# Hybrid RWKV-7 / RG-LRU / retention block: the projections alternate between two PSUM banks throughout the mixers

## Chip, core and metric

One NeuronCore of a Trainium2 chip runs the whole kernel as a single launch. The metric is the device time of one launch in microseconds (us), as a median over runs. The engines are named as in the profile: PE (TensorE; PEld is its weight load), DVE (VectorE), ACT (ScalarE), POOL (GpSimd) and SP (the sync engine, which here only issues DMAs).

## What is computed

One layer on 512 tokens of width 2048, in float32:

```python
h = rms_norm(x, norm1_g)
proj = h @ w_in                      # split by columns among three groups of heads
y_a = rwkv7_mixer(...)               # 12 heads x 64, delta-rule state, decay from the data
y_b = rglru_mixer(...)               # 512 channels, width-4 conv, gelu gate
y_c = retention_mixer(q, k, v, g, cos, sin, log_gamma, gn_g)   # 6 heads, qk 64, v 128, swish gate
x = x + concat(y_a, y_b, y_c) @ w_out
h = rms_norm(x, norm2_g)
x = x + (silu(h @ w_gate) * (h @ w_up)) @ w_down
return rms_norm(x, final_norm_g)
```

## The kernel before

**Precision and the unit of work.** Every large product is made in three matmuls: `split` (L157) writes a high half of an operand with ACT (the CAST of L158) and the rest with DVE (the TENSOR_TENSOR of L141), and `mm3` (L161) issues high by high, high by low and low by high as L162, L163 and L164. HH and HL are the two halves of h, resident in SBUF. Weights come through RAW (two slots of 128x1024, loaded by SP), and from there through WH and WL (four slots of 128x512 each).

**Projections.** `proj` (L270) makes one 128-column tile of `h @ w_in` for all 512 tokens: four weight pieces, 48 matmuls of 128x512 into one PSUM bank. The caller then reads the bank with DVE (`bank * rB`). Which bank it is, L272 decides. `ret_qk` (L731) makes the tiles cq and ck, `ret_gate` (L697) a tile cg.

**Value projections.** `ret_v` (L768), called with 0, 1 and 2, makes the values of two retention heads: 192 matmuls of 128x256, half of them into bank 0 and half into bank 7 (`vb`, L770). ACT then takes them out in eight activations of 128x128, four from each bank, into `vT`. With argument 0 these go to the slots 46 and 47 of the tile M; slot 46 also holds the decay table `DT[1]` (L721), which `ret_scores(1)` and its neighbours read on DVE. M, 45 slots of 128x512, holds nearly everything that the mixers keep.

**The third RWKV group.** `rwkv_inverse(2)` (L504) inverts 64 small triangular matrices with a chain of 62 dependent DVE instructions and a copy (L518), and passes the result through DRAM: SP writes scrN (L520) and scrX (L521) and reads them back into M (L523 and L530). `rwkv_join(2)` (L533) multiplies the parts with 32x32 matmuls on PE, with ACT copies between (L543, L552). `rwkv_chain(2)` (L556) then runs eight chunks, each a sequence from PE to DVE to PE to ACT and DVE to PE (L573, L145, L167, L581, L585, L594, L596, L600). The chunks hang on each other; other matmuls fill PE between their parts.

**What sets the order.** The steps are written in the order of the list SCHEDULE (L57). Its end reads: ... inverse 2, ..., qk 0, scores 0, join 2, qk 1, scores 1, chain 2, **value 0, qk 2**, out 2, heads 0, scores 2, **cg 4, value 1**, store 2, norm 0, **cg 5**, store 2 (first half), **value 2**, heads 1, ... From that order, from `tc.high_priority()` blocks and from which instructions it finds ready, a scheduler makes one list for each engine when the kernel is built. On the chip each engine works through its list in that order, and waits where an operand or a buffer isn't free. Within a bank the scheduler keeps a new group of matmuls behind the reads of the group before.

The two lines that decide the bank:

```python
o = bank[1 if ring["cv"] else nxt("proj", 2)]     # L272, in proj
ring["cv"] = 1                                    # first line of ret_v
```

So until `ret_v(0)` the tiles alternate between banks 0 and 1; from then on (cq 2, ck 2, cg 4, cg 5) all use bank 1, while the value projections use 0 and 7.

Of the kernel before, what the change touches and what calls it, by code (L numbers as in the profile page):

```python
# [98 lines left out]
def hybrid_block(ctx: ExitStack, tc: tile.TileContext, A: dict, out: bass.AP, dbg=None):  # L99
# [19 lines left out]
    bank = [pp.tile([128, 512], F32, name=f"bank{i}") for i in range(8)]  # L119
# [37 lines left out]
    def split(raw, hi, lo):  # L157
        S.copy(out=hi, in_=raw)  # L158
        tt(lo, raw, hi.bitcast(F32), SUB)

    def mm3(o, wh, wl, xh, xl, first, last, **kw):  # L161
        PE.matmul(o, wh, xh, start=first, stop=False, **kw)  # L162
        PE.matmul(o, wh, xl, start=False, stop=False, **kw)  # L163
        PE.matmul(o, wl, xh, start=False, stop=last, **kw)  # L164
# [24 lines left out]
    ring = {"sm": 0, "gn": 0, "raw": 0, "w": 0, "mm": 0, "proj": 0, "cv": 0}  # L189

    def nxt(k, n):
        v = ring[k]
        ring[k] = (v + 1) % n
        return v
# [74 lines left out]

    def proj(name, j, between=None):  # L270
        idx = W_IDX[(name, j)]
        o = bank[1 if ring["cv"] else nxt("proj", 2)]  # L272
        for half in range(2):
            with tc.high_priority() if idx > 1 else ExitStack():
                r = RAW[:, nxt("raw", 2), :]
                nc.sync.dma_start(out=r, in_=A["w_in"][idx, half])
                pcs = []
                for u in range(2):
                    w = nxt("w", 4)
                    split(r[:, u * 512:(u + 1) * 512], WH[:, w, :], WL[:, w, :])  # L280
                    pcs.append(w)
            if half and between:
                between()
            for u in range(2):
                w = pcs[u]
                for kk in range(4):
                    k = half * 8 + u * 4 + kk
                    cs = slice(kk * 128, (kk + 1) * 128)
                    mm3(o, WH[:, w, cs], WL[:, w, cs], HH[:, k, :], HL[:, k, :], k == 0, k == KT - 1)
        return o  # L290

    tok = []
    first = proj("k", 0, lambda: tok.append(head_rsqrt_stat(acc, c("mD"), 1, mmb, eps=NORM_EPS)))
    rT = drv[:, 108:112]
    V.tensor_copy(out=rT, in_=tok[0])
# [89 lines left out]
    def rwkv_proj(pr):  # L385
        sr, sk, sv = rkv(pr)
        with tc.high_priority() if pr > 1 else ExitStack():
            (G if pr else nc.sync).dma_start(out=LW, in_=A["lora"][pr, :, 0:256])
        shift(sk, proj("k", pr) if pr else first, "mu_k", pr)
        shift(sr, proj("r", pr), "mu_r", pr)  # L390
        shift(sv, proj("v", pr), "mu_v", pr)
# [967 lines left out]
```

## Time and profile before

| | us |
|---|---|
| median of 3 runs | 2301.12 (2299.13 to 2305.68) |
| the profiled execution | 2305.94 |
| its span, first to last instruction | 2304.0 |

The profile is of that one execution: a page with the busy time of each engine, and views of the trace by stretch, by line and in order of time. A row in order of time gives the start, the duration, the engine, the line, the operation, and in brackets the idle time ahead of it and what ended that. Matmuls overlap, so a matmul's duration is longer than its share of PE's time; the distance from start to start is what counts. A float32 matmul that isn't split (L167, L573, L596) leaves two records for one instruction. PEclk is the granted clock of TensorE; 1.00 is 2.4 GHz and 0.50 is 1.2 GHz.

### The profile page before, as it was taken

To read this page: it belongs to the slowest core of one execution; us is meant where nothing else is said; L and a number is where in the kernel's file an instruction comes from. 1 tells how busy PE (TensorE), PEld (TensorE's weight loads), DVE (VectorE), ACT (ScalarE), POOL (GpSimd) and SP (SyncE) were. 2 spreads that over 40 slices of the span, in tenths; PEclk is the share of its full clock that TensorE was granted. 3 is DMA by queue.
4 is the path that set the end of the run, shared out by engine and by line. 5 is a ranking of instruction groups with operands and counts; after the bars stand their busy time and mean duration, and the time that the engine had idled before them with its cause. 6 is when DMAs were issued, how large, how long until landed. Compare 5 with 4: busy or idle time off the path is not lost.

```text
span 2304.0 us, 29339 instructions
## 1 busy us (share of the span) xinstructions
PE 2261.3 (98%) x11005; PEld 1861.6 (81%) x11005; DVE 1632.9 (71%) x2749; ACT 1000.7 (43%) x1646; POOL 22.0 (1%) x59
## 2 busy tenths in 40 slices
PE   8999999999999999999999999999999999999998
PEld 7878777777888888788888888888888788888887
DVE  7778689688646554878777777878787455565555
ACT  5563465454225543444444444444444432232234
POOL 0000000000000000000000000000000000000000
PEclk9999999999989999999999999999999999999999
DMA  5324233324413454334333423342331544454332
GB/s 201 103 81 113 76 94 89 108 67 128 111 52 120 149 177 145 114 126 148 110 110 119 154 94 128 110 142 93 127 132 37 174 152 134 135 162 122 114 106 74
DMA packets 119070, 272.50 MB, mean 118 GB/s; under 512 B 35904, under 2 KB 42304, under 8 KB 107536
## 3 DMA queue, kind: packets, MB, share of 16 engines
q1 hardware_dynamic: 108208, 250.46, 34.5%
q10 hardware_dynamic: 8448, 12.59, 1.5%
q0 software_dynamic: 2272, 7.58, 1.1%
q8 instruction: 86, 1.41, 0.3%
q14 instruction: 56, 0.46, 0.1%
HBM read 241.36 MB, written 27.66 MB: 117 GB/s over the span
## 4 chain that ended last, share of the span: by engine, by line
PE 82%; DVE 13%; ACT 2%; issue 2%; DMA 1%; ACTq 0%; DVEq 0%; SPq 0%
PE bank L162 25%; PE bank L163 25%; PE bank L164 25%; PE bank L167 5%; DVE RB L141 4%; DVE WL L141 3%; DVE M L141 2%; DVE HL L141 1%; PE bank L573 1%; PE bank L1054 1%; DVE G L150 1%; PE bank L596 1%; DVE E L141 1%; ACT WH L158 1%; DVE M L150 0%
## 5 line engine op out<-in xcount | busy, mean ns | idle before, releaser
L162 PE MATMUL bank<-HH,WH 128*128 128x512 f32 x992 | 396.8, 400 | 13.4 <-ACT HH L153 5.8
L158 ACT CAST WH<-RAW 128x512 fp32r<-128x512 f32 (+1 forms) x339 | 216.9, 640 | 427.3 <-PE bank L163 365.7
L164 PE MATMUL bank<-HH,WL 128*128 128x512 f32 x992 | 394.4, 398 | 0.0
L163 PE MATMUL bank<-HL,WH 128*128 128x512 f32 x992 | 394.0, 397 | 0.0
L141 DVE TENSOR_TENSOR WL<-RAW,WH 128x512 fp32r<-128x512 f32 (+1 forms) x339 | 240.5, 710 | 130.5 <-ACT WH L158 126.7
L158 ACT CAST WH<-RB 128x1024 fp32r<-128x1024 f32 x191 | 201.2, 1055 | 269.4 <-PE bank L164 251.2
L141 DVE TENSOR_TENSOR WL<-RB,WH 128x1024 fp32r<-128x1024 f32 x191 | 233.1, 1221 | 110.9 <-ACT WH L158 109.7
L162 PEld LDWEIGHTS bank<-HH,WH 128*128 128x128 f32 x992 | 188.3, 190 | 53.4 <-ACT HH L153 5.8
L141 DVE TENSOR_TENSOR X<-X,bank 128x512 f32<-128x512 f32 (+1 forms) x178 | 115.9, 656 | 160.9 <-PE bank L164 159.9
L163 PE MATMUL bank<-GLo,WH 128*128 128x512 f32 x576 | 224.2, 389 | 0.0
L164 PE MATMUL bank<-GH,WL 128*128 128x512 f32 x576 | 224.2, 389 | 0.0
L162 PE MATMUL bank<-GH,WH 128*128 128x512 f32 x576 | 224.2, 389 | 0.0
L164 PEld LDWEIGHTS bank<-HH,WL 128*128 128x128 f32 x992 | 188.1, 190 | 38.9 <-issue 1.4
L163 PEld LDWEIGHTS bank<-HL,WH 128*128 128x128 f32 x992 | 188.3, 190 | 38.2 <-issue 1.4
L163 PE MATMUL bank<-WL,HH 128*128 128x512 f32 (+1 forms) x604 | 216.8, 359 | 0.0
L162 PE MATMUL bank<-WH,HH 128*128 128x512 f32 (+1 forms) x604 | 216.8, 359 | 0.0
L164 PE MATMUL bank<-WH,HL 128*128 128x512 f32 (+1 forms) x604 | 216.2, 358 | 0.0
L141 DVE TENSOR_TENSOR HL<-RB,HH 128x1024 fp32r<-128x1024 f32 (+2 forms) x127 | 128.6, 1027 | 56.5 <-ACT HH L158 55.7
L162 PE MATMUL bank<-WH,FAH 128*128 128x512 f32 x412 | 162.5, 395 | 3.8 <-ACT WH L158 3.8
L158 ACT CAST HH<-RB 128x1024 fp32r<-128x1024 f32 (+1 forms) x99 | 102.5, 1037 | 140.0 <-PE bank L164 126.7
L164 PE MATMUL bank<-WH,FAL 128*128 128x512 f32 x412 | 161.9, 393 | 0.0
L163 PE MATMUL bank<-WL,FAH 128*128 128x512 f32 x412 | 161.7, 392 | 0.0
(239 smaller groups left out, 3801.4 us busy)
## 6 DMA issues: line engine op xcount, KB each, us to landing
RB<-in_w_gu_dram SPq DMA_DIRECT2D x77, 1024.0 KB, 4.8
RAW<-in_w_in_dram SPq DMA_DIRECT2D x76, 512.0 KB, 3.6
RAW<-in_w_dn_dram SPq DMA_DIRECT2D x100, 256.0 KB, 2.7
RW<-in_w_dn_dram SPq DMA_DIRECT2D x76, 256.0 KB, 2.6
RAW<-in_w_out_dram SPq DMA_DIRECT2D x32, 512.0 KB, 3.6
RAW<-in_w_gu_dram SPq DMA_DIRECT2D x11, 1024.0 KB, 4.9
hscr<-H ACTq DMA_DIRECT2D x44, 256.0 KB, 2.2
FT<-hscr SPq DMA_DIRECT2D x40, 256.0 KB, 3.0
```

The source lines that it names most:

```text
L141: (eng or V).tensor_tensor(out=o, in0=a, in1=b, op=op)
L150: V.scalar_tensor_tensor(out=o, in0=a, scalar=s, in1=b, op0=op0, op1=op1, **kw)
L158: S.copy(out=hi, in_=raw)
L162: PE.matmul(o, wh, xh, start=first, stop=False, **kw)
L163: PE.matmul(o, wh, xl, start=False, stop=False, **kw)
L164: PE.matmul(o, wl, xh, start=False, stop=last, **kw)
L167: PE.matmul(o, l, r, start=start, stop=stop)
L573: PE.matmul(F[:, q, hv[e]], LS[e][:, ch, :], VS[:, ch, hv[e]], start=(q == 0 and e == 0), stop=True, skip_group_check=(q > 0 or e > 0))
L596: PE.matmul(F[:, q, :], P_[q][1][:, ch, :], ZBq[:, q, :], start=False, stop=True, skip_group_check=True)
L1054: PE.transpose(b[:, 128 * t:128 * t + 128], (G_, X_)[t // 2][:, t % 2, 128 * f:128 * f + 128], ident)
```

## The change

Projections always take the next of banks 0 and 1. `ring["cv"]` is still set, and nothing reads it any more.

```diff
     def proj(name, j, between=None):
         idx = W_IDX[(name, j)]
-        o = bank[1 if ring["cv"] else nxt("proj", 2)]
+        o = bank[nxt("proj", 2)]
         for half in range(2):
```

34 tiles are made ahead of `ret_v(0)`, an even number, so that now cq 2 takes bank 0, ck 2 bank 1, cg 4 bank 0 and cg 5 bank 1. No instruction is added or removed. The scheduler, though, makes other lists of them from the end of `ret_v(0)` to the end of the mixers. Up to there all lists are the same.

**Place 1, the end of the value projections of call 0.** In the rows, bank7 with 128x256 is the value projection, 128x512 with HH or HL first is a projection (bank1: cq 2, ck 2, cg 4), and 32x32 is `rwkv_join(2)`. PE's list before:

```order
L164 MATMUL bank7_88<-WH_77,HL_80 128x256
L162 MATMUL bank1_82<-HH_79,WH_77 128x512
L163 MATMUL bank1_82<-HL_80,WH_77 128x512
L164 MATMUL bank1_82<-HH_79,WL_78 128x512
...
L162 MATMUL bank7_88<-WH_77,HH_79 128x256
L163 MATMUL bank7_88<-WL_78,HH_79 128x256
...
L167 MATMUL bank3_84<-M_101 32x32 x8
L167 MATMUL bank2_83<-M_101 32x32 x8
```

Between the first and the last of these rows stand 144 matmuls into bank 1 (three whole tiles) and 4 of the value projection of call 1. PE's list now (zn, ZB and VSt are the chunk chain's tiles):

```order
L164 MATMUL bank7_88<-WH_77,HL_80 128x256
L167 MATMUL bank3_84<-M_101 32x32 x8
L167 MATMUL bank2_83<-M_101 32x32 x8
...
L167 MATMUL bank2_83<-M_101 128x128 x4
L167 MATMUL bank5_86<-zn_109,M_101 128x128
L167 MATMUL bank5_86<-M_101 128x128 x2
L162 MATMUL bank0_81<-HH_79,WH_77 128x512
L163 MATMUL bank0_81<-HL_80,WH_77 128x512
L164 MATMUL bank0_81<-HH_79,WL_78 128x512
L596 MATMUL bank4_85<-ZB_113,M_101 128x128 x2
L573 MATMUL bank6_87<-VSt_112,M_101 128x64 x4
```

The join follows the value projection directly. The 96 matmuls of cq 2 and ck 2 stand among the chunks of the chain, the 48 of cg 4 and all 192 of the value projection of call 1 behind the chain; before, 48 of the latter stood ahead of the chain, 140 within it and 4 behind. Six products of `ret_heads(0)` (64x128) and eight of `ret_scores(2)`, which stood among the first two chunks, stand behind the chain too, with three transposes (L760).

ACT's list now at the same place, with the activations that take `ret_v(0)`'s results out of banks 7 and 0:

```order
L158 CAST WH_77<-RAW_76 128x512 x5
L153 ACTIVATE M_101,SM_107<-bank7_88,drv_71 128x128 x4
L543 COPY M_101<-bank3_84 32x256
...
L552 ACTIVATE M_101<-bank2_83 32x8x32
L153 ACTIVATE M_101,SM_107<-bank0_81,drv_71 128x128 x2
...
L153 ACTIVATE M_101,SM_107<-bank0_81,drv_71 128x128 x2
L585 COPY ZB_113<-bank5_86 64x2x64 x2
```

Bank 7 is taken out ahead of the join's first copy, bank 0 among and behind the join's last ones. In the list of before the activations of bank 0 stand at the same place, with 12 more casts of weights (RAW to WH) ahead of the join.

**Place 2, the inverse.** The small DVE instructions `M<-M 64x...` are the inverse, `WL<-RAW,WH` are the splits of projection weights, and `M<-bank_82,rB` is the read of a finished tile. A piece of DVE's difference:

```order
 L141 TENSOR_TENSOR M<-M 64x11x21 x2
 L141 TENSOR_TENSOR M<-M 64x12x20 x2
-L141 TENSOR_TENSOR WL<-RAW,WH 128x512
 L141 TENSOR_TENSOR M<-M 64x13x19 x2
 L141 TENSOR_TENSOR M<-M 64x14x18 x2
-L141 TENSOR_TENSOR M<-M 64x15x17
-L141 TENSOR_TENSOR WL<-RAW,WH 128x512
-L141 TENSOR_TENSOR M<-M 64x15x17
+L141 TENSOR_TENSOR M<-M 64x15x17 x2
```

From the row 64x11x21 to the inverse's copy (L518), 13 instructions of 128x512 that belong to the projections (eight splits, two reads of banks, three of the rotary step) have left; nothing stands between the inverse's instructions there now.

SP's difference, from the reads of the inverse's input on (L276 and L774 load weights, L743 is the rotary step's shuffle):

```order
 L509 DMA M<-scrA 32x32x32 x2
-L276 DMA RAW<-in_w_in_dram 128x1024 x4
-L743 DMA M<-M 32x512
-L276 DMA RAW<-in_w_in_dram 128x1024
-L743 DMA M<-M 32x512 x3
-L774 DMA RAW<-in_w_cv_dram 128x1024
-L743 DMA M<-M 32x512
-L774 DMA RAW<-in_w_cv_dram 128x1024
+L276 DMA RAW<-in_w_in_dram 128x1024 x3
+L521 DMA scrX<-M 64x1024
 L520 DMA scrN<-M 32x1024
```

Behind L520 the list now goes on with the eight L530 and the two L523, where before two L774 and two more L743 stood among them. One L276 (first half of cg 4) and everything after it now comes behind the inverse's DMAs.

## Rows read from the trace of the kernel before

**Rows 1.** The page's head: span, and PE's busy time, share, instructions.

```profile
span 2304.0 us, 29339 instructions
PE 2261.3 (98%) x11005; PEld 1861.6 (81%) x11005; DVE 1632.9 (71%) x2749; ACT 1000.7 (43%) x1646; POOL 22.0 (1%) x59
```

**Rows 2.** Stretches: length; busy PE, PEld, DVE, ACT, POOL (instructions); PEclk, DMA, GB/s.

```profile
634.00:645.60 11.60, 9.46 (x90) 7.69 (x88) 3.15 (x7) 3.55 (x14) 0.00 (x0) 0.62 0.01 2
645.60:657.00 11.40, 11.40 (x49) 9.83 (x50) 5.67 (x15) 1.47 (x7) 0.00 (x0) 0.50 0.01 1
657.00:694.00 37.00, 36.57 (x277) 33.30 (x276) 19.73 (x57) 12.33 (x36) 3.74 (x7) 1.00 0.32 94
694.00:735.00 41.00, 40.92 (x277) 37.27 (x278) 30.37 (x94) 22.40 (x68) 2.67 (x5) 1.00 0.42 129
```

**Rows 3.** PE in order of time, around the third RWKV group.

```profile
566.14 1.15 PE L167 MATMUL bank<-M 64*128 64x128 f32 x8
...
589.24 0.28 PE L163 MATMUL bank<-WL,HH 128*128 128x256 f32 x1
589.36 0.28 PE L164 MATMUL bank<-WH,HL 128*128 128x256 f32 x1
589.48 0.40 PE L162 MATMUL bank<-HH,WH 128*128 128x512 f32 x1
...
602.21 0.47 PE L162 MATMUL bank<-HH,WH 128*128 128x512 f32 x1 [1.66 <-DVE M L141]
...
614.64 0.47 PE L162 MATMUL bank<-HH,WH 128*128 128x512 f32 x1 [1.30 <-DVE M L141]
...
625.61 0.28 PE L162 MATMUL bank<-WH,HH 128*128 128x256 f32 x1
...
626.17 1.19 PE L167 MATMUL bank<-M 32*32 32x32 f32 x32
...
645.60 1.22 PE L167 MATMUL bank<-M 128*128 128x128 f32 x4 [0.75 <-DVE M L581]
```

**Rows 4.** DVE in order of time, during the inverse.

```profile
590.83 0.68 DVE L141 TENSOR_TENSOR WL<-RAW,WH 128x512 fp32r<-128x512 f32 x1
...
601.38 0.69 DVE L141 TENSOR_TENSOR M<-bank,rB 128x512 f32<-128x512 f32 x1
601.98 0.68 DVE L141 TENSOR_TENSOR WL<-RAW,WH 128x512 fp32r<-128x512 f32 x1
...
615.25 1.11 DVE L518 COPY M<-M 32x1024 f32<-32x1024 f32 x1
616.29 0.54 DVE L141 TENSOR_TENSOR M<-M 128x384 f32<-128x384 f32 x1
```

**Rows 5.** DVE from 591.4 to 616.4 us, grouped by shape: count, busy, mean, idle.

```profile
L141 DVE TENSOR_TENSOR WL<-RAW,WH 128x512 fp32r<-128x512 f32 x9 | 6.1, 680 | 0.2 <-ACT WH L158 0.2
...
L141 DVE TENSOR_TENSOR M<-bank,rB 128x512 f32<-128x512 f32 x2 | 1.4, 684 | 0.0
L141 DVE TENSOR_TENSOR M<-M 128x512 f32<-128x512 f32 x2 | 1.4, 676 | 0.0
...
L141 DVE TENSOR_TENSOR M<-M,adT 128x512 f32<-128x512 f32 x1 | 0.7, 677 | 0.0
```

**Rows 6.** SP's DMA issues in order of time, behind the inverse of the first group.

```profile
224.46 0.48 SPq L521 DMA_DIRECT2D scrX<-M  x1
...
228.04 0.33 SPq L523 DMA_DIRECT2D M<-scrN  x1
```

**Rows 7.** Line L523, the reads of scrN: from issue to landing.

```profile
DMA to landing us min/median/max: 2.5/4.2/4.6
```

**Rows 8.** ACT in order of time: L585, once in each chunk of the chain.

```profile
646.86 0.55 ACT L585 COPY ZB<-bank 64x128 f32<-64x128 f32 x2 [1.10 <-PE bank L167]
...
658.35 0.53 ACT L585 COPY ZB<-bank 64x128 f32<-64x128 f32 x2
665.82 0.54 ACT L585 COPY ZB<-bank 64x128 f32<-64x128 f32 x2
...
693.19 0.54 ACT L585 COPY ZB<-bank 64x128 f32<-64x128 f32 x2 [2.37 <-PE bank L167]
```

## The prediction

> **What bounds the kernel now.** I read the page's head first: PE is busy for 98% of the span [rows 1], so time is lost only where PE stands or runs slowly, and a change that adds no instruction can only move such time. Then the table by stretch, around the place where the lists differ. PE's granted clock is 1.00 nearly everywhere, but 0.62 and then 0.50 from 634 to 657 us [rows 2], which is the level of 1.2 GHz: there PE has only the small products of the third RWKV group and little else to do. Then PE in order of time [rows 3]. The value projection of call 0 ends at 589.5 us. Behind it come 144 matmuls of 128x512 until 625.6 us, with two waits for a read of bank 1, of 1.66 and 1.30 us. These are the waits that a second bank would remove, 3.0 us together. At 626.2 us the join begins, at 645.6 us the chain's first state product. What matters most: while those 144 matmuls ran, DVE worked at the inverse (copy at 615.25 us [rows 4]), and PE needs the inverse only at 626.2 us. The projections were the cover of the inverse.
>
> **What the new lists do there.** cq 2 now goes to bank 0, and so behind the activations that take `ret_v(0)` out of bank 0. On ACT's list these stand at the join's end, in both kernels: they write the slot of M that holds a decay table, and on DVE's list the reads of that table stand behind the inverse. The scheduler therefore found cq 2 not ready, and with it ck 2 and cg 4, and put the join first. PE works its list in order, so it stands from the end of the value projection to the arrival of the inverse.
>
> **Term 1, the stall ahead of the join.** DVE's list is unchanged to the split at 590.83 us. Instructions of 128x512 start 0.60 us apart (601.38, 601.98 [rows 4]), so it goes on at 591.43 and reaches the copy's end at 616.29 us, in 24.9 us. From that 13 such instructions have left: eight of the nine splits (the ninth is the one at 590.83), two reads of a bank, three rotary ones [rows 5]. 13 x 0.60 = 7.8 us, and 0.2 us of waiting goes with them, so the copy runs from 607.2 to 608.3 us, 8 us sooner. Then the way through DRAM. In the first group, where nothing but a weight load stood between, L523 was issued 228.04 - 224.46 = 3.6 us behind L521, which left as the copy began [rows 6]; one more L530 is ahead of it now, so some 4.1 us, at 611.3. It lands 2.5 to 4.6 us later [rows 7]: the join can begin between 613.8 and 615.9 us; I take 614.7, the middle. PE stands from 589.5 to 614.7, for **25 us**, where it stood 3.0.
>
> **Term 2, from the join to the chain.** Before, 645.60 - 626.17 = 19.4 us [rows 3], in which 44 value matmuls stood too (5.3 us at 0.12, the distance of 589.24 and 589.36 [rows 3]). Now nothing stands among the join's products, but it waits on the same eight small DMAs, the same ACT copies, and at the low clock. Bounds 14.1 (19.4 less 5.3) and 19.4 us; I take 16, nearer to the row without the fillers, since SP's queue holds no weight load ahead of the L530. The first state product comes at 614.7 + 16 = 630.7 us, **14.9 us sooner** than before.
>
> **Term 3, the chain.** Before, 693.19 - 646.86 = 46.3 us from the first ZB copy to the last; the first two spacings 11.5 and 7.5, the other five 5.5 on average [rows 8]. The 14 products and three transposes of heads 0 and scores 2 that made the first spacing long have left (0.29 us each at full clock, by the four instructions at 566.14 [rows 3], and twice that at 1.2 GHz). In their place stand 12 to 13 projection matmuls in each spacing, 0.23 apart ((625.6 - 589.5 - 3.0) / 144 [rows 3]) or 0.46 at half clock, where 10 to 26 value matmuls stood. I estimate 8.2 and 7.6 for the first two and leave the others: 43.1, **3.2 us shorter**; bounds 6 us (both at 6.5, little above the later ones) and 0.
>
> **Term 4, the work behind the chain.** It grows by what the chain and the inverse no longer cover: 48 matmuls of cg 4 (11.0 us at 0.23), 188 more of value call 1 (22.6 at 0.12), the 14 products (4.1) and three transposes (0.4). **38.1 us**. Does something there stand that it could fill? From 694 to 735 us PE is busy for 40.9 of 41.0 us at full clock [rows 2], so almost nothing. The new wait there, call 1 of the value projections behind the read of cg 4 in bank 0, is covered by eight matmuls into bank 7 set ahead of it (1 us, against 1.3 to 1.7 for such a wait in [rows 3]): 0.5 us at most, left out. The splits for this work need 0.60 us of DVE for each 2.8 us of PE; the wait of ACT and DVE is no new bound.
>
> **The sum.** 38.1 - 14.9 - 3.2 = **+20.0 us**. The same by PE's own account: 25.2 - 3.0 of standing, and some 2 us less in join and chain together. Against the profiled execution (2305.94; span 2304.0) that is 2325.9; that execution lies 4.8 us above the median of 2301.12, to which the forecast is made: **2321**. By the ends of the terms: the join at 613.8, 14.1 us to the chain, and 6 us off it give 38.1 - 17.7 - 6 = +14.4; with 2 us of slack behind the chain +12. The join at 615.9, 19.4 us, and an equal chain give 38.1 - 10.3 = +27.8.
>
> **What a page says against this.** [Rows 3] show two waits of 3.0 us in all, each ended by DVE's read of bank 1. The Trainium skill's page "Perfetto Trace Analysis", section "Matmuls" under "Optimizing Tensor Performance", asks that independent groups of matmuls rotate through different PSUM banks, so that taking out one overlaps the next. By that rule this change is right and gives rival 1 its time; by the lists, the bank rotated to is one whose reader is late, and the rows above give +20.
>
> **Rivals.**
> 1. *Faster: only the waits go.* If the matmuls of cq 2 ran where they did, PE would save the two waits: 2301.1 - 3.0 = 2298. For it speaks that they are PE's only idle time from 589.5 to 625.6 us, against it that PE's list has no projection between the value projection and the join. That PE gets past a waiting product is shown nowhere in the trace. 2%, with all other ways to a gain beyond 0.3%.
> 2. *No change that can be measured.* The stall is paid back: the chain is a chain of latencies, and if its spacings fell to the 5.5 us of the later ones at once and the tail behind `ret_v(2)` had waits for the moved work to fill, +20 would shrink below 6.9 us (0.3%, about what a measurement of this kernel can tell from no change). It would take 13 us more than my terms give; all seven spacings at 5.5 give 4.6 of them. 5%, at about 2305.
> 3. *Slower still: the low clock stays.* Before, the clock rose at some 657 us [rows 2], amid value matmuls. If it stays at 1.2 GHz through the chain, the 12 matmuls of each of the last five spacings take 0.23 us more each, 5 x 2.8 = 14 us: 2335. Against it: PE had fillers among the chain's products then as it has now. 10%.
>
> **How the numbers follow.** The forecast of +12 to +28 (2313 to 2329) has 83%, rival 3 has 10, rival 2 has 5, rival 1 has 2. The range of 8 in 10 takes the forecast's own bounds and some of rival 3: 2312 to 2332. Slower by over 0.3%: 93%; within it 5%; faster 2%.
>
> **What would show it.** In the trace after: PE idle for about 25 us right behind the last 128x256 matmul at 589.5 us, ended by a DMA (M from scrN) or the join's weight load; L518 near 607 us instead of 615; the join near 615 and the chain's first ZB copy near 632; the clock at 0.50 from some time in the stall until past 640 us; the last ZB copy near 675; and the first matmuls of the output projection, which stand at the same places of the list, some 20 us later than before. What follows them should only be shifted. Wrong would be a stall below 20 us, or a distance from the last ZB copy to the output projection that grew by less than 34 us.

## Result and profile after

The kernel after takes 2321.07 us in the median (2320.46 to 2322.44), the kernel before, beside it, 2300.43 us (2299.13 to 2305.68): a ratio of 1.0081, 95% interval 1.0069 to 1.0092. The change costs 20.6 us; 2321.0 was forecast. The executions of the kernel before fall in two groups, near 2301 and near 2306 us, and the profile ahead of the prediction was of the upper (2305.94); the first experiment shows where these some 5 us lie.

The head of the page after, with PE's line and its clock in the 40 slices of the span (the counterpart of [rows 1]):

```profile
span 2318.8 us, 29344 instructions
PE 2254.1 (97%) x11005; PEld 1855.3 (80%) x11005; DVE 1636.5 (71%) x2749; ACT 1001.6 (43%) x1646; POOL 22.1 (1%) x59
PE   8999999999599999999999999999999999999998
PEclk9999999999699999999999999999999999999999
```

The same 11005 records of matmuls, but one slice, the eleventh, in which PE was busy for half of the time and its clock fell. PE in that slice in order of time (start, duration, engine, line, operation, what it waited for), with the first matmul of the output projection as the last row, the counterpart of [rows 3]:

```profile
587.75 0.28 PE L164 MATMUL bank<-WH,HL 128*128 128x256 f32 x1
613.51 4.10 PE L167 MATMUL bank<-M 32*32 32x32 f32 x80 [25.48 <-DMA M<-scrN]
...
629.21 1.22 PE L167 MATMUL bank<-M 128*128 128x128 f32 x4 [0.75 <-DVE M L581]
...
754.05 0.47 PE L162 MATMUL bank<-HH,WH 128*128 128x512 f32 x1
```

Behind the value projection the 144 matmuls of 128x512 are gone. PE stands for 25.48 us, until the inverse has come through DRAM, and the join follows without a value matmul in it. DVE in the same time, the counterpart of [rows 4]:

```profile
589.83 16.69 DVE L141 TENSOR_TENSOR M<-M 64x220 f32<-64x220 f32 x43
606.55 1.03 DVE L518 COPY M<-M 32x1024 f32<-32x1024 f32 x1
607.51 0.54 DVE L141 TENSOR_TENSOR M<-M 128x384 f32<-128x384 f32 x1
```

One row of 43 small instructions stands where the inverse was mixed with splits and reads of a bank, and the copy comes 18.8 us behind the last value matmul (606.55 - 587.75), where it was 25.9 (615.25 - 589.36 [rows 3, 4]). The last row is a read of the decay table DT[1], behind the inverse. By the order of ACT's list (place 1) it is bank 7 that is taken out behind it, at 608.08 us. Bank 0 waits longer, for the two reads of the table that make the scores, and their products stand in the join on PE's list. The second of these reads on DVE, the third of ACT's four activations that take out bank 0, and PE's first projection:

```profile
627.84 0.69 DVE L141 TENSOR_TENSOR M<-bank,M 128x512 f32<-128x512 f32 x1 [5.39 <-PE bank L167]
628.57 0.37 ACT L153 ACTIVATE M<-bank,drv 128x128 f32<-128x128 f32 x1 [2.51 <-DVE M L141]
630.08 0.77 PE L162 MATMUL bank<-HH,WH 128*128 128x512 f32 x1
```

So bank 0 is empty only at the end of the join, and the projections come behind it. Five stretches (columns as in [rows 2]): the stall, the join, the first 3.5 us of the chain, the rest of the chain, and the work from its last ZB copy to the output projection:

```profile
588.00:613.50 25.50, 0.03 (x1) 0.00 (x0) 18.47 (x50) 2.13 (x9) 0.00 (x0) 0.60 0.23 51
613.51:630.47 16.96, 14.81 (x156) 13.05 (x157) 2.82 (x6) 5.17 (x19) 0.00 (x0) 0.50 0.06 10
630.47:634.00 3.53, 3.53 (x16) 3.24 (x15) 1.58 (x5) 1.04 (x4) 0.00 (x0) 0.50 0.00 0
634.00:669.40 35.40, 35.40 (x210) 28.65 (x210) 22.20 (x62) 10.62 (x32) 3.75 (x7) 1.00 0.34 93
669.40:754.05 84.65, 84.65 (x597) 77.00 (x596) 46.59 (x118) 35.41 (x100) 2.68 (x5) 1.00 0.36 109
```

The clock is 0.50 (1.2 GHz) through the join and for 3.5 us of the chain, then 1.00. The 84.65 us behind the chain are full: nothing stands there that the moved work could fill. The ZB copies of the chain on ACT, the counterpart of [rows 8]:

```profile
630.47 0.55 ACT L585 COPY ZB<-bank 64x128 f32<-64x128 f32 x2 [1.09 <-PE bank L167]
637.39 0.55 ACT L585 COPY ZB<-bank 64x128 f32<-64x128 f32 x2
642.95 0.54 ACT L585 COPY ZB<-bank 64x128 f32<-64x128 f32 x2 [0.36 <-PE bank L167]
...
669.36 0.55 ACT L585 COPY ZB<-bank 64x128 f32<-64x128 f32 x2 [0.56 <-PE bank L167]
```

These rows cut the way from the last value matmul to the output projection into four pieces, and every kernel below is read by the same four (us, each from its own profile):

| kernel | to the join | to the first ZB copy | to the last ZB copy | to the output projection | sum |
|---|---|---|---|---|---|
| before, as shown ahead of the prediction | 36.8 | 20.7 | 46.3 | 45.0 | 148.8 |
| before, an execution of the lower group | 36.9 | 21.2 | 42.6 | 45.0 | 145.6 |
| forecast of after | 25.3 | 17.3 | 43.1 | 83.1 | 168.8 |
| after | 25.8 | 17.0 | 38.9 | 84.7 | 166.3 |
| odd_start | 29.9 | 17.0 | 40.7 | 72.5 | 160.1 |
| filled_stall | 25.4 | 16.6 | 39.4 | 84.7 | 166.1 |
| ck2_bank6 | 29.9 | 16.9 | 53.3 | 94.3 | 194.4 |
| own_table_one_bank | 38.4 | 22.7 | 38.4 | 39.4 | 138.9 |
| own_table_two_banks | 37.1 | 21.1 | 40.4 | 38.6 | 137.2 |

Beside an execution of the lower group, in which the medians of before lie, after is 20.7 us longer on this way, which is the whole of the 20.6 us. From the output projection to the end it is unchanged: 2318.8 - 754.05 = 1564.8 us, and 1564.6 in that execution of before (2299.0 - 734.37).

### The profile page after: what moved, and what is told of

It is laid out like the page before. It is cut to its first block, busy times and chain, and to the rows that moved or that the text cites. A ratio compares the mean times of both kernels' runs of the same rounds, so it can differ in the third digit from the quotient of the medians.

```text
span 2318.8 us, 29344 instructions
## 1 busy us (share of the span) xinstructions
PE 2254.1 (97%) x11005; PEld 1855.3 (80%) x11005; DVE 1636.5 (71%) x2749; ACT 1001.6 (43%) x1646; POOL 22.1 (1%) x59
## 4 chain that ended last, share of the span: by engine, by line
PE 82%; DVE 13%; ACT 2%; issue 2%; DMA 1%; SPq 0%; DVEq 0%; ACTq 0%
PE bank L163 25%; PE bank L162 25%; PE bank L164 25%; PE bank L167 4%; DVE RB L141 4%; DVE WL L141 3%; DVE M L141 2%; DVE HL L141 1%; PE bank L573 1%; PE bank L1054 1%; DVE G L150 1%; PE bank L596 1%; DVE E L141 1%; DVE M L150 0%; ACT WH L158 0%
```

## Experiments

### The kernel before twice more: where its two groups of times come from

No edit. What was expected of the two profiles:

> The kernel before, unchanged, profiled a second time. In the first two profiles the stretch from the end of value projection 0 to the output projection grew by only 17.5 us, while the medians lie 20.6 us apart and the profiled execution of before was 5.5 us above its own median. If that execution was only slow elsewhere, this profile again has 148.7 us from the value projection's end (589.48) to the output projection (738.19), within 1 us, and the difference lies in a shift of everything outside. If before's own stretch varies, it is shorter here, by up to 3 us, and the local loss is nearer to 20.6.

> The kernel before, unchanged, profiled a third time. Its executions fall in two groups, 2301.6 to 2302.1 (mean granted clock 0.993) and 2306.5 to 2306.9 (0.990), and both profiles so far are of the upper. If this one is of the lower, its stretches show where the 4.7 us lie: by theory in the join and chain of the third RWKV group, where the clock was 0.50 from 636 to 657 us and would rise sooner; by the rival in the stretches near 950 or 1810 us, where the clock also falls.

The first took 2305.93 us, again of the upper group, and repeats the profile shown ahead, with 148.9 us on the way. The second took 2300.95 us. First its ZB copies (compare [rows 8]: 646.86, 658.35, ..., 693.19), then three stretches of it:

```profile
646.80 0.54 ACT L585 COPY ZB<-bank 64x128 f32<-64x128 f32 x2 [1.09 <-PE bank L167]
654.52 0.53 ACT L585 COPY ZB<-bank 64x128 f32<-64x128 f32 x2
...
689.37 0.54 ACT L585 COPY ZB<-bank 64x128 f32<-64x128 f32 x2 [2.37 <-PE bank L167]
```

```profile
646.80:650.00 3.20, 3.20 (x19) 3.01 (x18) 1.72 (x6) 1.04 (x4) 0.00 (x0) 0.70 0.02 5
650.00:654.00 4.00, 4.00 (x35) 3.34 (x35) 3.12 (x8) 0.36 (x2) 0.00 (x0) 1.00 0.00 0
654.00:658.00 4.00, 4.00 (x29) 3.37 (x28) 2.31 (x7) 2.17 (x7) 0.00 (x0) 1.00 0.01 2
```

The same stretches in the profile shown ahead of the prediction:

```profile
646.80:650.00 3.20, 3.20 (x16) 2.86 (x14) 1.77 (x6) 1.04 (x4) 0.00 (x0) 0.50 0.02 5
650.00:654.00 4.00, 4.00 (x17) 3.33 (x17) 1.96 (x4) 0.00 (x0) 0.00 (x0) 0.50 0.00 0
654.00:658.00 4.00, 4.00 (x26) 3.45 (x25) 1.27 (x4) 0.54 (x2) 0.00 (x0) 0.59 0.00 0
```

The list is the same, and the first ZB copy comes within 0.06 us of the same time. But the clock rises between 646.8 and 650 us in the one and between 654 and 658 in the other, and the first spacing is 7.7 us instead of 11.5. That is 3.8 us of the 5.0 between the two executions, in the place that the theory named; 1.2 us are in what follows the output projection (1564.6 and 1565.8 us), and no other piece differs by more than 0.6 us. This rests on two profiles of the upper group and one of the lower.

### own_table_two_banks: the table apart, two banks kept

```diff
-    DT = [sl(45), sl(46), sl(45)]
+    DT1 = mp.tile([128, 384], F32, name="DT1")
+    DT = [sl(45), DT1, sl(45)]
```

> The kernel after, with two banks as there, but the second decay table (DT[1]) in a tile of its own instead of the slot of M that also holds the first value tile, vT[0]. ACT can then take bank 0 out without waiting for the table's readers behind the inverse. Theory (the stall comes from the late reader of bank 0): the 144 projection matmuls stand behind value projection 0 again, the stall of 25.5 us is gone, the last ZB copy to the output projection is back near 45 us, and the time is that of before, 2297 to 2302 us; the two waits of 1.66 and 1.30 us are gone, at most a wait of 3 us of the first of these matmuls for ACT's eight copies takes their place. Rival (the two banks themselves, or the bank that the chain meets later, cost the time): it stays at 2315 to 2321 us.

It took 2293.17 us, 0.9954 of before (0.9937 to 0.9971): the loss of 20.6 us is gone, and 8.9 us more. ACT takes bank 0 out in four activations. The first row is the third of them in the kernel before (its first two came at 640.08 and 640.43 us), the second is the first of them in this kernel:

```profile
644.95 0.37 ACT L153 ACTIVATE M<-bank,drv 128x128 f32<-128x128 f32 x1 [2.51 <-DVE M L141]
```

```profile
588.39 0.37 ACT L153 ACTIVATE M<-bank,drv 128x128 f32<-128x128 f32 x1 [1.50 <-PE bank L164]
```

The one was released by DVE, by the read of the table for the second head's scores at 644.23 us, some 55 us behind the value projection; the other by PE, by the value projection itself. (The read at 616.29 us [rows 4] is of the part of the slot that bank 7 goes to, and bank 7 was taken out right behind it.) In this kernel the read of the table comes as late as before, but nothing waits for it, since it is of another tile:

```profile
644.68 0.69 DVE L141 TENSOR_TENSOR M<-bank,DT 128x512 f32<-128x512 f32 x1 [1.50 <-PE bank L167]
```

With bank 0 free, the 144 projections stand behind the value projection again, and at this place the new turn costs one wait of the first of them:

```profile
589.95 0.50 PE L162 MATMUL bank<-HH,WH 128*128 128x512 f32 x1 [0.88 <-ACT M L153]
```

So the late reader of bank 0 is the cause of the loss, not the second bank. The extra gain was not expected. It shows in the stretch from the end of the projections into the chain, first of the kernel before (the execution of the lower group), then of this one:

```profile
616.00:646.00 30.00, 27.86 (x242) 24.07 (x241) 7.21 (x13) 9.05 (x30) 0.00 (x0) 0.82 0.33 88
```

```profile
616.00:646.00 30.00, 30.00 (x302) 27.23 (x301) 9.62 (x16) 8.03 (x17) 0.00 (x0) 1.00 0.48 120
```

The kernel before had only bank 7 for value call 1 inside the join, since bank 0 was still occupied there; now both are free, PE has no gap left in the join, and its clock doesn't fall. By the table the join is no shorter for it (21.1 us to the first ZB copy, and 21.2 before), but it holds 90 value matmuls instead of 46. Those 44 then no longer stand later: the chain and the work behind it are 2.2 and 6.4 us shorter.

### own_table_one_bank and own_table_two_banks_b: what the second bank is worth

The same two lines in the kernel before (one bank beside the value projections), and own_table_two_banks once more, on the same chip.

> The kernel before (one bank beside the value projections) with the second decay table in a tile of its own: the control for own_table_two_banks, which took 2293.17 us, 0.9954 of before. On its list the 144 projection matmuls stand in bank 1 behind value projection 0, and then call 1 of the value projections fills the join from both of its banks, where before's list has 37 and 7 of bank 7 only. Theory (the tile of its own frees bank 0 early, more value matmuls fill the join, and the granted clock stays at 1.00 there; the second bank is worth only the two waits of 1.66 and 1.30 us less the new one of 0.88): 2294 to 2297 us, the waits of some 1.6 and 1.3 us are still there, the clock between 636 and 657 us is above 0.9. Rival (the gain comes from the two banks): 2300 to 2303 us, the clock falls in the join as in the kernel before.

> The same kernel as own_table_two_banks, beside own_table_one_bank in one call, to measure what two banks are worth where the bank's reader is early. Theory: 2292.5 to 2295.6 as in its first call, 1 to 3 us below own_table_one_bank. Rival (two banks are worth nothing here, as the waits are filled by what DVE does): within 1 us of it.

One bank: 2293.60 us, 0.9963 of before (0.9951 to 0.9976). Two banks: 2292.60 us, 0.9958 (0.9946 to 0.9970). Nearly all of the gain comes from the table's own tile: with one bank (0.4 us below the range expected) the two waits are still there, and the join is full at full clock, by PE's rows and one stretch of own_table_one_bank:

```profile
602.30 0.56 PE L162 MATMUL bank<-HH,WH 128*128 128x512 f32 x1 [1.89 <-DVE M L141]
...
616.13 0.47 PE L162 MATMUL bank<-HH,WH 128*128 128x512 f32 x1 [1.11 <-DVE M L141]
```

```profile
616.00:650.00 34.00, 33.87 (x314) 30.16 (x315) 12.62 (x24) 8.62 (x18) 0.00 (x0) 1.00 0.42 106
```

The two medians are 1.0 us apart, and the ranges of the times overlap (2293.11 to 2295.42 with one bank, 2292.52 to 2293.47 with two), so the second bank is worth about a microsecond here, and hardly clear of the noise. That lies on the border between the theory and the rival. By the rows it removes waits of 1.89 and 1.11 us and brings one of 0.88, which would be 2.1; but with two banks a new wait stands behind the chain, where value call 2 comes close behind the taking of call 1, and with it the waits are even (3.00 and 3.19 us). The row is of PE in own_table_two_banks_b:

```profile
697.16 0.39 PE L162 MATMUL bank<-WH,HH 128*128 128x256 f32 x1 [2.31 <-ACT M L153]
```

own_table_two_banks is the fastest of these kernels, below the kernel before by some 9 us.

### odd_start: a third of the cover back

The kernel after, with the turn beginning at the other bank:

```diff
     def ret_v(pi):
+        if not ring["cv"]:
+            ring["proj"] = 1
         ring["cv"] = 1
```

> The kernel after, but the turn of the two banks begins with bank 1 at the first retention head: cq 2 and cg 4 go to bank 1, ck 2 and cg 5 to bank 0. Only cq 2 is then independent of ACT's late copies: 48 of the 144 matmuls (11 us at 0.23) stand again between value projection 0 and the join. Theory: the stall ahead of the join shrinks from 25.5 to 12 to 16 us (the inverse gets a few splits of DVE's in its way again), and about 11 us of the loss come back less what the chain is worth: 2307 to 2313 us. Rival (the loss is not in the uncovered inverse but in the chain or the work behind it): the stall shrinks, but the time stays within 3 us of 2321.

It took 2317.02 us, 1.0056 of before (1.0041 to 1.0071). Of the 20.6 us only 4 to 6 came back (4.1 by the medians, 5.7 if each is taken against before beside it, 6.2 by the table), where 11 us of cover had been put back: the forecast of 2307 to 2313 was wrong. The stall was 18.70 us, not 12 to 16. PE's row of the join, and DVE during the inverse:

```profile
619.26 4.10 PE L167 MATMUL bank<-M 32*32 32x32 f32 x80 [18.70 <-DMA M<-scrN]
```

```profile
601.40 0.69 DVE L141 TENSOR_TENSOR M<-bank,rB 128x512 f32<-128x512 f32 x1
602.01 0.68 DVE L141 TENSOR_TENSOR WL<-RAW,WH 128x512 fp32r<-128x512 f32 x1
...
612.40 1.02 DVE L518 COPY M<-M 32x1024 f32<-32x1024 f32 x1
```

The cover brings its own splits, a read of its bank and a rotary product (at 609.79 us), and all of these go to DVE, the engine that the inverse runs on: the join begins 4.1 us later than in after (29.9 and 25.8 in the table). Of the 12.2 us that leave the end (84.7 to 72.5), 4.1 are lost there and 1.8 in the chain.

### filled_stall: the stall filled with work for PE alone

The kernel after, with 100 matmuls in the stall:

```diff
+    def warm(n):
+        for i in range(n):
+            PE.matmul(bank[1], HH[:, i % KT, 0:128], HH[:, i % KT, :], start=(i == 0), stop=(i == n - 1))
...
         steps[kind](j)
+        if (kind, j) == ("cv", 0):
+            warm(100)
```

> The kernel after, with 100 more matmuls of 128x512 into bank 1, whose result nobody reads, placed on PE's list between value projection 0 and the join: 100 x 0.23 = 23 us of added work in the stall of 25.5 us. It tells the price of the low clock behind the stall apart from the price of standing. Theory: the wait ahead of the join falls to 1 to 4 us, the join still begins within 1 us of where it did (24 to 26 us behind the value projection), and with the granted clock at 0.90 or more from there on, join to first state product takes 13 to 15 us instead of 15.7 and the first two spacings of the chain's ZB copies 5.3 to 6 instead of 6.92 and 5.56; the time falls by 2 to 5 us, to 2316 to 2319. Rival (the clock costs nothing there, as latencies set the join and chain): the time is that of after, 2320 to 2322. If the added matmuls delay the join, it is more.

It took 2322.11 us, 1.0077 of before (1.0062 to 1.0092): the time of after. PE, then three stretches (the filled stall, the join, and the first 3.45 us of the join alone):

```profile
589.27 22.86 PE L535 MATMUL bank<-HH 128*128 128x512 f32 x100
614.55 0.62 PE L167 MATMUL bank<-M 32*32 32x32 f32 x14 [2.42 <-DMA M<-scrN]
```

```profile
589.27:614.55 25.28, 22.86 (x103) 18.59 (x101) 18.71 (x50) 2.13 (x9) 0.00 (x0) 1.00 0.24 50
614.55:631.14 16.59, 14.44 (x156) 12.68 (x157) 2.83 (x6) 5.16 (x19) 0.00 (x0) 0.53 0.08 13
614.55:618.00 3.45, 3.45 (x79) 3.45 (x80) 0.00 (x0) 1.44 (x4) 0.00 (x0) 0.63 0.38 60
```

22.9 us of matmuls cost nothing: the inverse on DVE, and no work of PE, sets when the join begins. My theory of the clock failed. It was 1.00 to the join's start, through a wait of 2.42 us too, and fell within the first 3.45 us of the join all the same; in the mean of the join it was 0.53, and the join took 16.6 us instead of 17.0. So the stand of 25 us isn't needed for the fall. The wait of 2.42 us ahead of the join and the join's own small products aren't told apart by this run; in the profile of before shown ahead of the prediction the clock fell between 636 and 640 us (0.60 in the mean), behind the last value matmul of the join (633.85 us) and two waits of PE of only 0.46 us. So the run doesn't price a join at full clock without fillers, and that price stays open.

### ck2_bank6: one projection to another late bank

The kernel before, with ck 2 alone sent elsewhere:

```diff
-        o = bank[1 if ring["cv"] else nxt("proj", 2)]
+        o = bank[(6 if (name, j) == ("ck", 2) else 1) if ring["cv"] else nxt("proj", 2)]
```

> The kernel before with a single projection, ck 2, sent to bank 6 instead of bank 1; the turn of two banks isn't in it. Bank 6 is used by the chain of the third RWKV group (the products of VSt), so its list has cq 2 (48 matmuls in bank 1) behind value projection 0, then the join and the chain without projections, and ck 2 and cg 4 behind the chain. Theory (what costs is any projection that has to wait for a bank behind the inverse, since those behind it on the list go with it): a stall of 15 to 20 us ahead of the join, as the 18.70 us of odd_start, and a time 12 to 25 us above before. Rival (it is bank 0, the value projections' own, that matters): within 3 us of before.

It took 2350.86 us, 1.0210 of before (1.0195 to 1.0226), 49 us more and twice the upper end of what was expected. The stall ahead of the join is as expected, but in the chain, with no projection beside its products, ACT stands for some 5 us ahead of most ZB copies, and the clock doesn't rise until the chain's end. PE's row of the join, the ZB copies, and the stretch of the chain:

```profile
618.43 4.10 PE L167 MATMUL bank<-M 32*32 32x32 f32 x80 [18.70 <-DMA M<-scrN]
```

```profile
635.38 0.54 ACT L585 COPY ZB<-bank 64x128 f32<-64x128 f32 x2 [1.09 <-PE bank L167]
...
651.54 0.54 ACT L585 COPY ZB<-bank 64x128 f32<-64x128 f32 x2 [4.93 <-PE bank L167]
658.87 0.54 ACT L585 COPY ZB<-bank 64x128 f32<-64x128 f32 x2 [4.94 <-PE bank L167]
```

```profile
635.00:689.00 54.00, 41.74 (x163) 34.95 (x162) 16.69 (x58) 7.88 (x31) 3.73 (x7) 0.50 0.11 35
```

From the second on the spacings are 7.3 us at 0.50 (the last 7.8, with its copy at 688.63 us), where those of after, with projections between and at full clock, are 5.3 to 6.4 and the last 3.9. The chain takes 53.3 us and covers nothing, and all that it covered stands behind it: 94.3 us to the output projection instead of 45.0. By the table: 7.0 and 4.2 us sooner at the join and the first ZB copy, 10.7 and 49.3 longer behind, +48.8. I had priced the stall and forgotten what the chain covers. It isn't bank 0 that matters, but any bank that comes free late: bank 6, which the chain itself uses, costs more.

## Why the prediction was right, and where it was not

**The mechanism** (the projections wait for a bank that is emptied behind the inverse, the cover goes, PE stands) is shown by the 25.48 us wait and by own_table_two_banks, in which only the two value banks are made free early and the loss is gone; own_table_one_bank shows what the tile of its own does without the change.

**Term 1**, the stall: 25.2 us forecast, 25.48 measured. Its parts had small opposite errors: the copy began 18.8 us behind the last value matmul, 17.8 forecast, and the way through DRAM took 7.0 us from there (613.51 - 606.55), 7.5 forecast.

**Term 2**, join to first state product: 16 us forecast, 15.70 measured (629.21 - 613.51). The row without fillers was the right end to lean to, although the clock was low throughout.

**Term 3**, the chain, is the term that was mis-sized. Forecast were 43.1 us, measured 38.9; the first two spacings were 6.9 and 5.6 us, not 8.2 and 7.6, and the clock was 1.00 from 634 us on, not past 640 as the signs had it; the last ZB copy came at 669.36 us, not near 675. The shortening by 7.4 us lies outside the bounds given (0 to 6). The failing step is to take the first spacing of [rows 8], 11.5 us, for a property of the kernel: the third profile has 7.7 there with the same list. Against that execution the chain is 3.7 us shorter, and 3.2 was forecast.

**Term 4**, the work behind the chain: +38.1 us forecast, +39.7 measured (84.7 - 45.0). The lists show the difference: behind the last ZB product stand 55 more matmuls of 128x512 (115 against 60), where I counted the 48 of cg 4. The seven others, at 0.23, are the 1.6 us. The 188 value matmuls were counted rightly.

**The sum** hit the median to 0.1 us by luck, by two steps that cancel. Against the profiled execution of before the way grew by 17.5 us, not 20.0: term 3 missed by 4.2, term 4 by 1.6 the other way. I then took the 4.8 us by which that execution lies above the median as something outside the terms, and added +20 to the median. Most of them lay in term 3 itself. Against a profile of the lower group the terms read: 11.1 us sooner at the join, 4.2 between join and first ZB copy, 3.7 in the chain, 39.7 later behind it, +20.7.

**The rivals.** Rival 1, that only the waits go, would have needed the projections in place; own_table_two_banks puts them there, and the waits are indeed gone, but they are worth 1.0 us beside one bank with the same table. The Trainium skill's page "Perfetto Trace Analysis", section "Matmuls", has independent groups rotate through banks; the runs agree, if at all, only where the bank rotated to is emptied early: 1.0 us gained there, hardly clear of the noise, against 20.6 lost. Rival 2, payback, came true in one of its halves, since the chain's spacings fell to 5.56 us in the mean (38.9 / 7); the other half is excluded by the filled 84.65 us behind the chain. Rival 3, the low clock staying through the chain, did not come about in after, where projections stand among the chain's products; in ck2_bank6, where none do, it did, at 0.50 to the chain's end.

**What stays open.** Why the clock rises some 8 us later in one execution of the same list than in another, what a full clock would save in a join without fillers, and whether the second bank's 1.0 us is more than noise.

## What to carry to other kernels

Before a second bank is given to a producer, follow the bank's reader back: what it writes to, who still reads that memory, and where on the engines' lists that reading stands; a slot shared with a table that was read late made the second bank cost 20.6 us here, and a tile of its own made the same change harmless and the kernel 9 us faster than before, 8 of them without the change. Work that covers another engine's long job is worth its length less what it puts on that engine: 11 us of projections bought 4 to 6. And when the runs of a kernel fall into two groups, find out which group the profile is of before terms are taken from it.

## What the hardware showed

- With the same list and the same start within 0.06 us, PE's granted clock rose from 0.50 (1.2 GHz) to 1.00 (2.4 GHz) between 646.8 and 650 us in one execution and between 654 and 658 in another. This makes 3.8 us of the 5 between the two groups of times. The Trainium skill's page "TensorE: Matmul & The Clock Gate", section "Part 1: The HAM clock gate", says that the point at which the clock rises varies from run to run of one kernel, by half a microsecond either way in its example; the traces agree that it varies, but by some 8 us.
- 100 matmuls at full clock ahead of the join, and a wait of 2.42 us, did not keep the clock up in it: 1.00 until 614.55 us, 0.53 in the mean of the 16.6 us after (filled_stall). Value matmuls among the join's products did (1.00 from 616 to 646 us in own_table_two_banks).
- A chain of small products (128x128 and 128x64) without fillers stayed at 0.50 for 54 us, although PE counted as busy for 41.7 of them (ck2_bank6).
